# Copies of cache rows issued beside the weights' loads: in all four stages, or in the two feed-forward stages alone

## The chip, the cores and the metric

The kernel runs on one core of a Trainium2 chip. The metric is the device time of one execution in microseconds (us). The core's engines work side by side, each through its own list of instructions in order: TensorE (PE in the profile, its weight loads PEld), VectorE (DVE), ScalarE (ACT), GpSimd (POOL) and SyncE (SP), which here issues every DMA.

## What is computed

One inference step of a two-layer decoder, in float32: 512 new tokens of a prompt and one new token for each of 8 sample sequences, 520 columns in all, model width 1024.

```python
for i in range(DEPTH):                 # 2 layers
    x += mixer[i % 2](rmsnorm(x))      # 0: gated DeltaNet, 1: dilated window attention
    x += square(relu(rmsnorm(x) @ w_up)) @ w_down
# outputs: x, new states, and the key/value caches moved on by one row
bufs.append(jnp.concatenate([buf, new_rows], axis=1)[:, -keep:])
```

The last line is what the change is about. The sample sequences' caches (windows of 128, 512 and 1024 rows, 8 sequences, 8 KB a row) are outputs too: all old rows but the dropped one go unchanged from an input in DRAM to an output in DRAM, and one new row is added to each.

## The kernel before

The program has four stages in a row: `gdn` (the gated DeltaNet mixer), `mlp0` (feed-forward), `dsw` (dilated attention), `mlp1` (feed-forward). Activations stay on the chip with the model dimension on the partitions. Every projection takes a weight tile of 512 KB from DRAM (`raw`, L145, three buffers), which ScalarE rounds to `whi` (L130) and VectorE subtracts to `wlo` (L131), two buffers each; TensorE then runs three matmuls for each of the 8 blocks of the contraction (L164 to L166), in two halves of 260 columns, each in one of two PSUM buffers `mm`. A half is read out by an eviction (L762 and L896 are two of them) before its buffer is used again. A tile is thus 48 matmuls.

The copies of cache rows are a generator, `kept_rows` (L87): each is one DMA from DRAM to DRAM of up to 104 rows (832 KB; the rests are 704, 760 and 184 KB), 136 in all. After every weight load, `weights` draws from it:

```python
nc.sync.dma_start(raw, c[:, j : j + m].rearrange("(k p) n -> p k n", p=P))
self.owed += PACE[self.stage]
while self.owed >= 1:
    self.owed -= 1
    next(self.kept, None)
```

`owed` starts at -16, so the first 16 loads have no copy beside them, and every later one has one until the 136 are issued. After the last stage `for _ in K.kept: pass` (L1369) issues what is left, before the output is stored (`store_x`, L311).

In `gdn` the work goes by 8 pairs of heads, p = 0 to 7. For each pair a matrix has to be inverted. `decay` makes it on VectorE (E, L603). `invert` writes E's 32x32 blocks to DRAM (L629, four DMAs), loads them in another layout (Ft, L632), runs 31 steps of two small instructions on GpSimd (L638, L641), writes the result (L642) and loads it back (L646, four DMAs, into the tile `held`). `merge` joins the blocks, and begins on VectorE:

```python
nc.vector.transpose(T64[0:32, :, 0:32], Uf[0:32, :, 0:32])            # L653
nc.vector.transpose(T64[32:64, :, 32:64], Uf[32:64, :, 32:64])
nc.vector.transpose(T2[64:96], Uf[64:96, :, 64:96])
```

While that runs, the pair before is scanned (L713 to L743), its gates are projected (two tiles, evicted at L762), and its sample part (sks L820, sut L830, son L846) and its normalised output (osb L866, then otr L871) are made; `out_proj` (evicted at L896) adds earlier pairs to x. The order of instructions on each engine isn't the written one: a scheduler makes it, from a model of each instruction's and DMA's time; functions marked `urgent` and the DMAs in them come first where they can.

Of the kernel before, what the change touches and what calls it, by code (L numbers as in the profile page):

```python
# [43 lines left out]
MM = 2  # L44
OHB = 8
DOUT = {8: ((0,), (1, 2))}
PACE = dict(gdn=1, mlp0=1, dsw=1, mlp1=1)


class Common:  # L50


    def __init__(self, ctx, tc, I, O):
        self.tc, self.nc, self.I, self.O = tc, tc.nc, I, O
        nc = self.nc
        self.cst = ctx.enter_context(tc.tile_pool(name="cst", bufs=1))
        self.wp = ctx.enter_context(tc.tile_pool(name="wp", bufs=3))
        self.tp = ctx.enter_context(tc.tile_pool(name="tp", bufs=2))
        self.dp = ctx.enter_context(tc.tile_pool(name="dp", bufs=2, space=DRAM))
        self.pm = ctx.enter_context(tc.tile_pool(name="pm", bufs=2, space=PSUM))  # L60

        n = KT * T
        base = self.cst.tile([P, n + 2 * P + 4 * KT + SMALL], F32, name="base")
        split = self.cst.tile([P, 2 * n], F32R, name="split")
        self.x, self.xh, self.xl = (t.rearrange("p (k t) -> p k t", k=KT) for t in (base[:, :n], split[:, :n], split[:, n:]))
        self.ident, self.ones = base[:, n : n + P], base[:, n + P : n + 2 * P]
        self.gains = base[:, n + 2 * P : n + 2 * P + 4 * KT]
        self.small, self.places, self.used = base[:, n + 2 * P + 4 * KT :], {}, 0
        make_identity(nc, self.ident)
        nc.vector.memset(self.ones, 1.0)  # L70
        self.kept, self.owed, self.stage = self.kept_rows(), -16, "gdn"
        self.gain = {}
        for i, n in enumerate(("norm_mix", "norm_mlp")):
            self.gain[n] = self.gains[:, i * 2 * KT : (i + 1) * 2 * KT].rearrange("p (l k) -> p l k", l=2)
# [58 lines left out]
    def weights(self, cols, nk=KT):  # L133
# [4 lines left out]
        for c in cols:  # L138
            for j in range(0, c.shape[1], step):
# [5 lines left out]
# [3 lines that stand above are left out]
# [1263 lines left out]
```

## Time and profile before

| | us |
|---|---|
| median of 3 runs | 2148.9 (2146.82 to 2150.51) |
| the profiled execution, its own time | 2152.49 |
| its span, from the first to the last instruction | 2150.7 |
| TensorE busy in the span | 1972.8 (92%) |
| VectorE busy | 1319.7 (61%) |
| ScalarE busy | 892.5 (41%) |
| GpSimd busy | 500.4 (23%) |

By its first and last DMAs, `gdn` ends at about 790 us, `mlp0` at about 1130, `dsw` at about 1765, and `mlp1` goes to the end. The copies are issued from 153.9 to 1280.5 us: 49 in `gdn`, 64 in `mlp0`, 23 in `dsw`. To read the profile: a busy share is an average over stages with different limits, so the stretches are read one by one; an engine's idle time is put down to what ended it ("<-"); the granted clock of TensorE was 0.954 of full speed over the span.

### The profile page before, as it was taken

The page shows a single profiled execution, that of the slowest core. Times are in us where ns is not written, and L with a number is a line of the kernel's source. Part 1 is how long each engine was busy: PE and PEld are TensorE (multiplying, and loading weights), DVE is VectorE, ACT ScalarE, POOL GpSimd, SP SyncE. Part 2 cuts the span into 40 slices and gives each one's busy share as a digit, 9 for nine tenths or more (in the row PEclk, how much of TensorE's full clock was granted, in tenths as well). Part 3 has the DMA queues.
Part 4 walks back from the last instruction along what each step waited for, and adds up shares of the span by engine and source line. Part 5 has one row for each costly group of instructions (what it writes and reads, how often), then busy time and mean ns, then how long its engine had stood idle before and what let it go on. Part 6 is the DMA issues. An engine that isn't in the chain of part 4 may idle for free. (4 is left out here: it accounts for less than half of the span.)

```text
span 2150.7 us, 41729 instructions
## 1 busy us (share of the span) xinstructions
PE 1972.8 (92%) x16436; PEld 1937.4 (90%) x16436; DVE 1319.7 (61%) x3301; ACT 892.5 (41%) x2391; POOL 500.4 (23%) x749
## 2 busy tenths in 40 slices
PE   8959867977968789999999999999999989999998
PEld 7858867977968689999999999999999989999998
DVE  4746766956956575454454667666766784454444
ACT  4525433444434352323244545554555443233231
POOL 1162334444344230000001223322332340000000
PEclk8979988989989789999999999999999999999999
DMA  5534554746844538766765774453454333333332
GB/s 139 101 88 134 145 134 135 225 142 167 250 136 134 190 113 281 253 232 230 251 232 204 240 235 131 119 149 99 119 136 133 114 96 89 98 89 91 97 89 70
DMA packets 416277, 328.55 MB, mean 153 GB/s; under 512 B 48408, under 2 KB 404568, under 8 KB 413896
## 3 DMA queue, kind: packets, MB, share of 16 engines
q1 hardware_dynamic: 416080, 325.88, 50.4%
q8 instruction: 129, 2.11, 0.4%
q14 instruction: 68, 0.56, 0.1%
HBM read 302.19 MB, written 132.83 MB: 202 GB/s over the span
## 5 line engine op out<-in xcount | busy, mean ns | idle before, releaser
L164 PE MATMUL mm<-split,whi 128*128 128x260 f32 (+1 forms) x2960 | 861.7, 291 | 22.0 <-DVE base L848 17.4
L166 PE MATMUL mm<-split,wlo 128*128 128x260 f32 (+1 forms) x2960 | 849.1, 287 | 20.3 <-DVE wlo L131 20.3
L165 PE MATMUL mm<-split,whi 128*128 128x260 f32 (+1 forms) x2960 | 846.5, 286 | 1.1 <-DVE split L178 1.1
L164 PEld LDWEIGHTS mm<-split,whi 128*128 128x128 f32 (+1 forms) x2960 | 564.2, 191 | 24.5 <-DVE base L848 17.5
L166 PEld LDWEIGHTS mm<-split,wlo 128*128 128x128 f32 (+1 forms) x2960 | 563.1, 190 | 23.3 <-DVE wlo L131 22.5
L165 PEld LDWEIGHTS mm<-split,whi 128*128 128x128 f32 (+1 forms) x2960 | 564.3, 191 | 2.1 <-DVE split L178 1.5
L130 ACT CAST whi<-raw 128x1024 fp32r<-128x1024 f32 (+1 forms) x273 | 285.4, 1045 | 503.5 <-PE mm L165 484.2
L131 DVE TENSOR_TENSOR wlo<-raw,whi 128x1024 fp32r<-128x1024 f32 (+1 forms) x273 | 336.5, 1233 | 196.9 <-ACT whi L130 188.0
L166 PE MATMUL mm<-hh,wlo 128*128 128x260 f32 x1024 | 289.1, 283 | 0.0
L165 PE MATMUL mm<-hl,whi 128*128 128x260 f32 x1024 | 288.4, 282 | 0.0
L164 PE MATMUL mm<-hh,whi 128*128 128x260 f32 x1024 | 287.9, 282 | 0.0
L165 PEld LDWEIGHTS mm<-hl,whi 128*128 128x128 f32 x1024 | 192.7, 188 | 0.0
L166 PEld LDWEIGHTS mm<-hh,wlo 128*128 128x128 f32 x1024 | 192.6, 188 | 0.0
L164 PEld LDWEIGHTS mm<-hh,whi 128*128 128x128 f32 x1024 | 192.3, 188 | 0.0
L346 DVE TENSOR_TENSOR t<-mm,bc 128x260 f32<-128x260 f32 x128 | 54.8, 428 | 153.1 <-PE mm L166 153.1
L190 POOL TENSOR_TENSOR acc<-acc,sq 128x260 f32<-128x260 f32 x42 | 37.0, 889 | 380.3 <-ACT sq L189 379.9
L638 POOL TENSOR_TENSOR fs<-Ft,held 128x60 f32<-128x60 f32 (+24 forms) x248 | 90.3, 364 | 112.1 <-DMA Ft<-D 93.4
L130 ACT CAST hh<-q 128x260 fp32r<-128x260 f32 x128 | 52.5, 410 | 121.6 <-DVE q L333 121.6
L641 POOL TENSOR_TENSOR held<-held,fs 128x60 f32<-128x60 f32 (+24 forms) x248 | 90.4, 364 | 19.4
L131 DVE TENSOR_TENSOR hl<-q,hh 128x260 fp32r<-128x260 f32 x128 | 54.9, 429 | 57.1 <-ACT hh L130 57.1
L164 PE MATMUL mm<-onh,whi 128*128 128x260 f32 x256 | 85.2, 336 | 2.8 <-DVE ET L618 2.2
L839 POOL TENSOR_TENSOR ub<-ub,base 128x1024 f32<-128x1024 f32 x16 | 32.7, 2044 | 216.7 <-DMA ub<-Du 201.6
(378 smaller groups left out, 3273.9 us busy)
## 6 DMA issues: line engine op xcount, KB each, us to landing
out_dram<-in_cache_kv_w_dram SPq DMA_DIRECT2D x112, 832.0 KB
raw<-in_dsw_w_in_dram SPq DMA_DIRECT2D x72, 512.0 KB
raw<-in_mlp_w_up_dram SPq DMA_DIRECT2D x64, 512.0 KB
raw<-in_mlp_w_down_dram SPq DMA_DIRECT2D x64, 512.0 KB
raw<-in_gdn_w_in_dram SPq DMA_DIRECT2D x48, 512.0 KB
S<-in_state_gdn_dram SPq DMA_DIRECT2D x16, 512.0 KB
raw<-in_gdn_w_out_dram SPq DMA_DIRECT2D x16, 512.0 KB
ub<-Du SPq DMA_DIRECT2D x16, 512.0 KB
```

The costliest lines, as they stand in the source:

```text
L130: nc.scalar.copy(hi, src)
L131: nc.vector.tensor_tensor(lo, src, hi.bitcast(F32), ALU.subtract)
L164: nc.tensor.matmul(ps[:m], lhsT=w[0][:, k, :m], rhs=xh[:, s], start=k == 0, stop=False)
L165: nc.tensor.matmul(ps[:m], lhsT=w[0][:, k, :m], rhs=xl[:, s], start=False, stop=False)
L166: nc.tensor.matmul(ps[:m], lhsT=w[1][:, k, :m], rhs=xh[:, s], start=False, stop=k == nk - 1)
L190: nc.gpsimd.tensor_tensor(acc[:, s], acc[:, s], t, ALU.add)
L346: nc.vector.tensor_tensor(t, ps, r2[:, s], ALU.mult)
L638: nc.gpsimd.tensor_tensor(tmp[:, :m, :n], Ft[:, None, j + 1 :, j].to_broadcast([P, m, n]), Uo[:, :m, j : j + 1].to_broadcast([P, m, n]), A ...
L641: nc.gpsimd.tensor_tensor(Uo[:, :m, j + 1 :], Uo[:, :m, j + 1 :], tmp[:, :m, :n], ALU.add)
L839: nc.gpsimd.tensor_tensor(ub, ub, kqs[:, :, 0:1].to_broadcast([P, NS, P]), ALU.mult)
```

## The change

Two numbers change. `gdn` and `dsw` draw no copies, and `owed` starts at 0.

```diff
-PACE = dict(gdn=1, mlp0=1, dsw=1, mlp1=1)
+PACE = dict(gdn=0, mlp0=1, dsw=0, mlp1=1)
...
-        self.kept, self.owed, self.stage = self.kept_rows(), -16, "gdn"
+        self.kept, self.owed, self.stage = self.kept_rows(), 0, "gdn"
```

The two feed-forward stages have 64 loads each, so 128 copies are issued beside loads and 8 at the end. The scheduler makes another order from this, on all engines. Three places follow.

SP at the end of the program, before the change (`raw` is a weight tile, `yt` a block of the output):

```order
L145 DMA raw<-in_mlp_w_up_dram 128x8x128 x8
L145 DMA raw<-in_mlp_w_down_dram 128x8x128 x8
L311 DMA out_dram<-yt 128x1024 x4
L311 DMA out_dram<-yt 8x1024
L1407 UNCONDITIONAL_BRANCH
```

and now:

```order
L145 DMA raw<-in_mlp_w_down_dram 128x8x128
L97 DMA out_dram<-in_cache_kv_w_dram 16x13312 x7
L311 DMA out_dram<-yt 128x1024
L97 DMA out_dram<-in_cache_kv_w_dram 16x13312
L311 DMA out_dram<-yt 128x1024
L97 DMA out_dram<-in_cache_kv_w_dram 16x11264
L311 DMA out_dram<-yt 128x1024 x2
L311 DMA out_dram<-yt 8x1024
```

Seven copies now follow the last load, and two more stand between the stores of the output.

VectorE in `gdn`, at the merge of pair 7 (`sz<-zt,mm` is the eviction of a gate half, `wlo` a weight split), before:

```order
L844 TENSOR_TENSOR base<-base 128x16
L762 SCALAR_TENSOR_TENSOR sz<-zt,mm 128x260
L848 TENSOR_SCALAR base<-son 128x16
...
L131 TENSOR_TENSOR wlo<-raw,whi 128x1024
L219 TENSOR_TENSOR base<-base 128x24
L762 SCALAR_TENSOR_TENSOR sz<-zt,mm 128x260
L653 STREAM_TRANSPOSE held<-held 32x8x32
L654 STREAM_TRANSPOSE held<-held 32x8x32
```

and now:

```order
L823 TENSOR_TENSOR base<-base,held 128x8
L653 STREAM_TRANSPOSE held<-held 32x8x32
L826 TENSOR_TENSOR base<-base 128x16
L654 STREAM_TRANSPOSE held<-held 32x8x32
L827 TENSOR_TENSOR base<-base 128x16
L762 SCALAR_TENSOR_TENSOR sz<-zt,mm 128x260
L655 STREAM_TRANSPOSE T_7894<-held 32x256
L844 TENSOR_TENSOR base<-base 128x16
L131 TENSOR_TENSOR wlo<-raw,whi 128x1024
```

The transposes of the merge have moved ahead of the sample part's last steps, of a weight split and of both evictions.

VectorE at the merge of pair 5 (`base<-base,mm` is an eviction of the output projection), before:

```order
L896 TENSOR_TENSOR base<-base,mm 128x260
L827 TENSOR_TENSOR base<-base 128x16
L844 TENSOR_TENSOR base<-base 128x16
L896 TENSOR_TENSOR base<-base,mm 128x260 x2
L848 TENSOR_SCALAR base<-son 128x16
L653 STREAM_TRANSPOSE held<-held 32x8x32
```

and now:

```order
L896 TENSOR_TENSOR base<-base,mm 128x260
L653 STREAM_TRANSPOSE held<-held 32x8x32
L827 TENSOR_TENSOR base<-base 128x16
L654 STREAM_TRANSPOSE held<-held 32x8x32
L896 TENSOR_TENSOR base<-base,mm 128x260
L844 TENSOR_TENSOR base<-base 128x16
L655 STREAM_TRANSPOSE T_6151<-held 32x256
L896 TENSOR_TENSOR base<-base,mm 128x260
L131 TENSOR_TENSOR wlo<-raw,whi 128x1024
```

Here L653 has moved ahead of L844 and of two evictions. In pair 3 it moves ahead of one weight split and one eviction L762, in pair 6 ahead of L728, L596, L743, four small instructions and two evictions L896; in pair 4 it moves behind L844 and one weight split, and there E stands behind one weight split and three convolution steps (L525) that it stood ahead of. In pairs 0, 1 and 2 it keeps its place.

## Rows read from the trace of the kernel before

**Rows 1.** Busy time in four stretches: us, PE, PEld, DVE, ACT, POOL (instructions); PEclk, DMA share, GB/s

```profile
150.00:300.00 150.00, 119.92 (x1032) 115.77 (x1033) 94.56 (x282) 61.59 (x180) 57.19 (x129) 0.85 0.51 134
...
850.00:900.00 50.00, 50.00 (x420) 50.00 (x420) 24.57 (x43) 15.17 (x26) 0.00 (x0) 1.00 0.68 238
...
1200.00:1250.00 50.00, 49.96 (x416) 49.35 (x414) 30.89 (x98) 27.41 (x90) 18.31 (x11) 1.00 0.81 244
...
1850.00:1900.00 50.00, 50.00 (x420) 50.00 (x419) 23.50 (x42) 17.09 (x31) 0.00 (x0) 1.00 0.33 96
```

**Rows 2.** Who waited for whom: us in total, times, longest

```profile
DVE held L653 <- DMA held<-D: 91.0, 7, 19.6
```

**Rows 3.** VectorE in order of time, L653 of pairs 3, 5, 6, 7: start, us

```profile
371.92 0.43 DVE L653 STREAM_TRANSPOSE held<-held 32x256 f32<-32x256 f32 x1 [9.95 <-DMA held<-D]
...
535.81 0.43 DVE L653 STREAM_TRANSPOSE held<-held 32x256 f32<-32x256 f32 x1 [14.13 <-DMA held<-D]
...
617.54 0.43 DVE L653 STREAM_TRANSPOSE held<-held 32x256 f32<-32x256 f32 x1 [18.54 <-DMA held<-D]
...
702.30 0.43 DVE L653 STREAM_TRANSPOSE held<-held 32x256 f32<-32x256 f32 x1 [11.19 <-DMA held<-D]
```

**Rows 4.** TensorE in order of time, after its idle time in pairs 3 to 7

```profile
377.21 1.97 PE L871 MATMUL otr<-base,osb 128*128 128x128 f32 x8 [8.93 <-DVE osb L866]
...
452.15 0.58 PE L846 MATMUL son<-base 128*128 128x16 f32 x2 [11.57 <-DVE base L844]
...
538.93 0.58 PE L166 MATMUL mm<-split,wlo 128*128 128x260 f32 x1 [11.37 <-DVE wlo L131]
...
619.64 0.38 PE L830 MATMUL sut<-base 128*16 128x128 f32 x1 [18.04 <-DVE base L823]
...
706.28 1.97 PE L871 MATMUL otr<-base,osb 128*128 128x128 f32 x8 [12.44 <-DVE osb L866]
```

**Rows 5.** SP's DMA issues in order of time, pairs 1, 3 and 6

```profile
138.98 0.56 SPq L632 DMA_DIRECT2D Ft<-D  x1
...
325.70 1.82 SPq L629 DMA_DIRECT2D D<-E  x4
327.62 0.40 SPq L145 DMA_DIRECT2D raw<-in_gdn_w_in_dram  x1
328.06 0.59 SPq L97 DMA_DIRECT2D out_dram<-in_cache_kv_w_dram  x1
328.89 0.60 SPq L632 DMA_DIRECT2D Ft<-D  x1
...
558.20 2.37 SPq L796 DMA_DIRECT2D S<-in_state_gdn_dram  x2
562.35 2.69 SPq L629 DMA_DIRECT2D D<-E  x4
...
568.19 0.59 SPq L632 DMA_DIRECT2D Ft<-D  x1
```

**Rows 6.** GpSimd in order of time, the first step on Ft of pairs 1, 3, 6

```profile
148.79 0.25 POOL L638 TENSOR_TENSOR fs<-Ft,held 128x31 f32<-128x31 f32 x1 [9.53 <-DMA Ft<-D]
...
338.56 0.26 POOL L638 TENSOR_TENSOR fs<-Ft,held 128x31 f32<-128x31 f32 x1 [8.74 <-DMA Ft<-D]
...
580.55 0.25 POOL L638 TENSOR_TENSOR fs<-Ft,held 128x31 f32<-128x31 f32 x1 [12.99 <-DMA Ft<-D]
```

**Rows 7.** VectorE in order of time, weight splits ahead of L653, pairs 3 and 7

```profile
360.10 1.23 DVE L131 TENSOR_TENSOR wlo<-raw,whi 128x1024 fp32r<-128x1024 f32 x1 [2.38 <-ACT whi L130]
...
689.39 1.23 DVE L131 TENSOR_TENSOR wlo<-raw,whi 128x1024 fp32r<-128x1024 f32 x1 [0.16 <-ACT zt L761]
```

**Rows 8.** SP's DMA issues at the end

```profile
2091.09 17.73 SPq L145 DMA_DIRECT2D raw<-in_mlp_w_down_dram  x4
2142.35 4.08 SPq L311 DMA_DIRECT2D out_dram<-yt  x5
```

**Rows 9.** Busy time of one stretch at the end, columns as in rows 1

```profile
2144.00:2146.00 2.00, 1.00 (x10) 0.57 (x7) 1.37 (x2) 0.89 (x2) 0.00 (x0) 1.00 1.02 408
```

## The prediction

> **What bounds the kernel now.** I read the time by stage first, then who waits for whom, then single stretches in order of time.
>
> By stage: in the feed-forward stages TensorE never stops. A stretch of 50 us holds 420 matmuls, 0.119 us each, both in the first feed-forward stage, where a copy goes out beside each load, and in the second, where none does [rows 1]. The DMA engines are 0.68 busy there with copies and 0.33 without, and nobody waits. The first stage (gated DeltaNet, some 790 us) is different: TensorE is busy 119.92 of 150 us in the row shown [rows 1]. What is won or lost must be looked for there, and at the very end.
>
> Waits of the first stage: VectorE waits 91.0 us, seven times, for `held<-D` at L653 [rows 2]. L653 is the first instruction of a pair's merge. Before it lies a chain: E (VectorE), four writes to DRAM (L629), the load of Ft (L632), 62 small GpSimd steps, a write (L642), four loads (L646). VectorE takes its instructions in order, so whatever stands behind L653 waits too, and TensorE soon runs dry. At L653 of pairs 3, 5, 6 and 7 the waits are 9.95, 14.13, 18.54 and 11.19 us [rows 3]; TensorE's idle times in pairs 3 to 7 are 8.93, 11.57, 11.37, 18.04 and 12.44 us [rows 4]: 62 us. So a pair lasts as long as its chain, plus the work that the order puts between L653 and the next E. Two things change it: how long the chain takes, and what stands ahead of L653.
>
> **The change part by part.**
>
> *The chain without copies.* 49 copies leave the first stage. What they cost the chain is bounded by the chain's own transfers. From Ft's issue to the first GpSimd step it takes 9.67 us in pair 3 (328.89 to 338.56), with a weights' load and a copy issued just before it; 9.81 us in pair 1 (138.98 to 148.79), before the first copy of the kernel; and 12.36 us in pair 6 (568.19 to 580.55), the longest of pairs 1 to 7 [rows 5, 6]. From the first write of E to Ft's issue it is 3.19 us in pair 3 and 5.84 in pair 6 [rows 5]. Lower bound: pairs 1 and 3 say a copy costs nothing, 0. Upper bound: six pairs, all as bad as pair 6, and copies the only reason: 6 x (2.69 + 2.65) = 32 us. The mean between pair 3 and pair 6 over six pairs is 16; but in pair 6 two loads of state, 512 KB each, are issued 4 us ahead of E [rows 5], and they stay. I take half, **-8 us**. What follows, 33.4 us in pair 3 from the first GpSimd step to L653 (338.56 to 371.92) [rows 3, 6], is GpSimd's steps for the most part and stays.
>
> The Trainium skill (DMA: Bandwidth & Descriptors, "Queues, rings and completion order") has each DMA engine consume the descriptors of a queue in ring order, so a Ft issued behind a copy would start only after it. Pair 3 against pair 1 does not show that, pair 6 may. By the rule, with one copy of 2.1 us (priced below) ahead of Ft in each of pairs 3 to 7, this term would be -10.5, and the total 2.5 us lower.
>
> *The order of work.* Nothing in the diff says so, but the order on VectorE is made by a scheduler that reckons with the DMA queue, and without copies it puts L653 earlier in pairs 3, 5, 6 and 7 and later in pair 4. Where it is earlier, work that kept TensorE going during the chain now waits for it. `mm` has two PSUM banks, so TensorE gets two halves beyond the last eviction that stands ahead of L653. With t0 the start of L653:
> - Pair 7. Before, the weight split wlo (start 689.39) and two evictions L762 stand ahead of L653 [rows 7], TensorE finishes both gate tiles and waits only at `otr`, from 693.84 to t0 + 3.98 [rows 3, 4]. Now they stand behind: 48 matmuls (2 halves of 24, 5.7 us) cannot run. wlo is the eighth instruction from L653 on, ready at about t0 + 3.5 (eight durations of 0.2 to 1.2 us), and 5.7 us later `otr` comes: t0 + 9.2, so +5.2.
> - Pair 5. Before, TensorE waits from 527.56 to t0 + 3.12 for wlo. Now L844 and two evictions L896 stand behind L653. It stops after 12 matmuls of the output projection, at about 521.0, and 6.5 us of matmuls (55) follow after about t0 + 1.4: t0 + 7.9, so +4.8.
> - Pair 6. Eight instructions with 3.4 us in all (among them L596, 1.3 us) and two evictions come behind L653; TensorE stands 12 matmuls earlier and gets to `sut` at t0 + 5.5 in place of t0 + 2.10: +3.4.
> - Pair 3. wlo (360.10) and one L762 come behind L653 [rows 7]; 46 matmuls, 5.5 us, follow from t0 + 2.5: t0 + 8.0 in place of t0 + 5.29: +2.7.
> - Pair 4. L844 and wlo come ahead of L653, which frees some 12 matmuls (-1.3), but E itself moves behind one wlo and three convolution steps, up to 4 us of VectorE; between -1.3 and +2.7 I take +1.
>
> Sum **+17 us**. Bounds: 0, if what moved runs while VectorE would have kept TensorE waiting anyway; +19 with pair 4 at its worst. I take it nearly whole, as TensorE has no other long idle time after these waits to catch up in.
>
> *The dilated-attention stage* loses 23 copies. In a stretch of it in which they run, TensorE is busy 49.96 of 50 us [rows 1], so there is nothing to win: **0**; the order there changes by a few places, which I bound by 2 us either way, one gap of TensorE of the smallest kind in [rows 3, 4] (L653 to `sut`, 2.10).
>
> *The second feed-forward stage* gets 64 copies. The first one has the same load and copy pattern and the same 420 matmuls in 50 us [rows 1]: **0**. The cover is the DMA engines' free third; if it were gone, the loads would come late at wlo.
>
> *The end.* 136 copies, 128 loads: eight copies have no load. One copy goes beside the last load (the load ends at 2108.8 on SP) and six follow it, 33 us before the first store of the output [rows 8]: done by then, as 7 x 2.1 us is 15. Two stand between the stores of the output on SP. The price of a copy: (238 - 96) GB/s for (0.68 - 0.33) of the engines [rows 1], so 406 GB/s with all; 832 KB take 2.1 us, 704 KB 1.8. The stores are issued from 2142.35 on [rows 8], and in their last microseconds the engines are full, 1.02 at 408 GB/s [rows 9]. So the two copies delay the end by 3.9 us; not below 0, and with 2 us for their own landing at most 6. **+4 us**.
>
> Sum: -8 + 17 + 0 + 0 + 4 = +13. The profiled execution took 2152.49 us (its span 2150.7, and 1.8 around it), so 2165.5; the median shown is 3.6 lower, which gives **2162 us**.
>
> **Rivals.**
> - *The moved work costs nothing (faster).* What moves behind L653 runs beside VectorE's square roots up to L866, in which TensorE waits 2.1 to 5.3 us now. For: that wait is real [rows 3, 4]. Against: the moved work is 5.5 to 6.5 us in three pairs, more than that wait. The point from which it decides: a moved work of no more than these 2.1 to 5.3 us a pair, with a chain gain above 8 us. With a gain of 12, between my 8 and the mean of 16: -12 + 0 + 4 = -8, 2141 us.
> - *The chain gets as short as the scheduler reckons (no change).* If the copies were all of pair 6's excess, the waits shrink by 20 to 25 us in all, which pays for +17 and +4: 2145 to 2149 us. The skill's ring order, at full effect on L629 and Du as well, points this way. Against: pair 3.
> - *The copies hold up the second feed-forward stage (slower still).* A load behind a copy comes late at its split. It decides once the DMA engines have no free time left. Against: the equal 420 matmuls [rows 1]. Were each of the 64 splits that follow late by a tenth of a copy's 2.1 us, that is 13 us more: 2175.
>
> **How the numbers follow.** This kernel's runs can tell about 0.2%, 4.3 us, from no change. The forecast, slower by 13, has 0.6, and the third rival 0.05: slower 0.65. The second rival and the small sums around it: 0.18 same. The first: 0.17 faster. The range reaches down to 2144, where the chain gains most of its bound, and up to 2174, with the moved work at +19, the chain at 0 and the end at 6.
>
> **What would show it.** Right: VectorE's waits at L653 of pairs 3, 5, 6 and 7 longer than before, with TensorE idle about 14 us or more there; Ft still 9.5 to 11 us from issue to GpSimd; 420 matmuls per 50 us in both feed-forward stages; the end some 4 us later after the last eviction. Wrong: Ft and L629 faster by 3 us a pair; L653 waits under 8 us; or matmuls of the second feed-forward stage waiting for wlo.

## The result, and the profile after

| | us | against the kernel before, 95% interval |
|---|---|---|
| before, median | 2147.95 (2146.82 to 2150.51) | |
| the change, median | 2158.84 (2157.68 to 2160.51) | 1.0050 [1.0032, 1.0067] |
| the change, profiled execution | 2158.45, span 2156.7 | |

Slower by 0.5%, 10.9 us between the medians. The two profiled spans lie only 6.0 apart, because the profiled execution of before was itself 4.5 above its median; so single traces are used below for where time goes, and medians for how much.

**By stage.** The same instruction in both traces, first of before, then of the change: the first eviction of the first feed-forward stage (L333), and weight splits (L131) late in that stage, early in the second feed-forward stage and at its end (columns: start, duration, engine, line, operation, output and input, idle time ahead of it and what ended it):

```profile
785.60 0.42 DVE L333 SCALAR_TENSOR_TENSOR q<-mm,r 128x260 f32<-128x260 f32 x1
...
1163.16 1.23 DVE L131 TENSOR_TENSOR wlo<-raw,whi 128x1024 fp32r<-128x1024 f32 x1 [2.43 <-ACT whi L130]
...
1808.18 1.23 DVE L131 TENSOR_TENSOR wlo<-raw,whi 128x1024 fp32r<-128x1024 f32 x1 [2.04 <-ACT whi L130]
...
2130.22 1.23 DVE L131 TENSOR_TENSOR wlo<-raw,whi 128x1024 fp32r<-128x1024 f32 x1
```

```profile
792.98 0.42 DVE L333 SCALAR_TENSOR_TENSOR q<-mm,r 128x260 f32<-128x260 f32 x1
...
1170.79 1.23 DVE L131 TENSOR_TENSOR wlo<-raw,whi 128x1024 fp32r<-128x1024 f32 x1 [2.44 <-ACT whi L130]
...
1808.34 1.23 DVE L131 TENSOR_TENSOR wlo<-raw,whi 128x1024 fp32r<-128x1024 f32 x1 [1.11 <-PE mm L166]
...
2131.55 1.22 DVE L131 TENSOR_TENSOR wlo<-raw,whi 128x1024 fp32r<-128x1024 f32 x1
```

The change is 7.4 us behind when the first stage is over, 7.6 at the end of the first feed-forward stage, 0.2 after the attention stage, 1.3 at the last split. The first stage loses, the feed-forward stages keep their pace, the attention stage gives back (how much of that is the change is measured below), and the rest of the 6.0 comes behind the last split.

The feed-forward stages of the change, both with a copy beside each load now (window view; columns as in [rows 1]):

```profile
850.00:900.00 50.00, 50.00 (x420) 50.00 (x419) 24.20 (x42) 13.32 (x20) 0.00 (x0) 1.00 0.67 234
1850.00:1900.00 50.00, 50.00 (x420) 50.00 (x419) 24.32 (x43) 16.58 (x30) 0.00 (x0) 1.00 0.70 247
```

420 matmuls in 50 us in both, as in [rows 1]: 64 more copies hold nothing up there.

**The first stage.** VectorE's waits at L653 of pairs 3 to 7 in the change; [rows 3] has four of them before:

```profile
370.45 0.43 DVE L653 STREAM_TRANSPOSE held<-held 32x256 f32<-32x256 f32 x1 [13.18 <-DMA held<-D]
...
452.76 0.43 DVE L653 STREAM_TRANSPOSE held<-held 32x256 f32<-32x256 f32 x1 [16.00 <-DMA held<-D]
...
534.38 0.43 DVE L653 STREAM_TRANSPOSE held<-held 32x256 f32<-32x256 f32 x1 [15.57 <-DMA held<-D]
...
613.96 0.43 DVE L653 STREAM_TRANSPOSE held<-held 32x256 f32<-32x256 f32 x1 [16.55 <-DMA held<-D]
...
697.22 0.43 DVE L653 STREAM_TRANSPOSE held<-held 32x256 f32<-32x256 f32 x1 [14.30 <-DMA held<-D]
```

And TensorE's idle times there, which answer to [rows 4]:

```profile
373.22 0.58 PE L166 MATMUL mm<-split,wlo 128*128 128x260 f32 x1 [8.10 <-DVE wlo L131]
...
454.42 0.62 PE L786 MATMUL sst<-base 128*128 128x24 f32 x2 [14.23 <-DVE base L848]
...
536.04 0.61 PE L846 MATMUL son<-base 128*128 128x16 f32 x2 [13.99 <-DVE base L844]
...
619.10 0.38 PE L830 MATMUL sut<-base 128*16 128x128 f32 x1 [15.62 <-DVE base L823]
...
699.53 0.58 PE L846 MATMUL son<-base 128*128 128x16 f32 x2 [12.01 <-DVE base L844]
```

Pair 4's, which [rows 3] does not have, was 13.93 us before, and its L653 started at 450.84. So VectorE waits longer at L653 in four pairs of five (not in pair 6), although every L653 but pair 4's starts earlier than before. TensorE's idle time is 64.0 us against 62.4 [rows 4]: hardly more. So the lost 7 us are not in these waits alone.

**The end.** SyncE from the first store on (answering to [rows 8]):

```profile
2143.82 0.36 SPq L311 DMA_DIRECT2D out_dram<-yt  x1
2144.22 0.51 SPq L97 DMA_DIRECT2D out_dram<-in_cache_kv_w_dram  x1
2144.84 0.60 SPq L311 DMA_DIRECT2D out_dram<-yt  x1
2145.49 0.51 SPq L97 DMA_DIRECT2D out_dram<-in_cache_kv_w_dram  x1
2146.11 1.86 SPq L311 DMA_DIRECT2D out_dram<-yt  x3
```

From the first store to the end of the span it is 12.9 us (2143.82 to 2156.7), before 8.35 (2142.35 to 2150.7): +4.5.

### The profile page after: what moved, and what is told of

The parts are those of the page before. It is cut to its first block, busy times and chain, and to the rows that moved or that the text cites. A ratio compares the mean times of both kernels' runs of the same rounds, so it can differ in the third digit from the quotient of the medians.

```text
span 2156.7 us, 41701 instructions
## 1 busy us (share of the span) xinstructions
PE 1973.8 (92%) x16436; PEld 1941.1 (90%) x16436; DVE 1323.4 (61%) x3301; ACT 895.6 (42%) x2391; POOL 500.6 (23%) x749
## 3 DMA queue, kind: packets, MB, share of 16 engines
q1 hardware_dynamic: 416080, 325.88, 50.7%
## 5 line engine op out<-in xcount | busy, mean ns | idle before, releaser
L164 PEld LDWEIGHTS mm<-split,whi 128*128 128x128 f32 (+1 forms) x2960 | 564.6, 191 | 26.6 <-DVE base L848 20.2
L131 DVE TENSOR_TENSOR wlo<-raw,whi 128x1024 fp32r<-128x1024 f32 (+1 forms) x273 | 342.8, 1256 | 154.9 <-ACT whi L130 111.2
L131 DVE TENSOR_TENSOR hl<-q,hh 128x260 fp32r<-128x260 f32 x128 | 54.9, 429 | 57.0 <-ACT hh L130 57.0
L839 POOL TENSOR_TENSOR ub<-ub,base 128x1024 f32<-128x1024 f32 x16 | 34.2, 2138 | 204.1 <-DMA ub<-Du 160.4
```

Of the source, the lines that this page charges most:

```text
L131: nc.vector.tensor_tensor(lo, src, hi.bitcast(F32), ALU.subtract)
L164: nc.tensor.matmul(ps[:m], lhsT=w[0][:, k, :m], rhs=xh[:, s], start=k == 0, stop=False)
L839: nc.gpsimd.tensor_tensor(ub, ub, kqs[:, :, 0:1].to_broadcast([P, NS, P]), ALU.mult)
```

## The experiments

"The run without copies at the end" is e3, the base of several others.

**The parts alone: e1, e2, e3, e5.** The first stage alone (e1): copies by a count for each stage.

```diff
-PACE = dict(gdn=0, mlp0=1, dsw=0, mlp1=1)
+LEFT = dict(gdn=0, mlp0=64, dsw=23, mlp1=49)
...
-                self.owed += PACE[self.stage]
-                while self.owed >= 1:
-                    self.owed -= 1
-                    next(self.kept, None)
+                if self.left[self.stage] > 0:
+                    self.left[self.stage] -= 1
+                    next(self.kept, None)
```

> No copies in the first stage, but the 23 copies of the attention stage stay where they were (beside its first 23 loads), 64 beside the first feed-forward stage's loads, 49 beside those of the second, none after the last load. Forecast theory (the chain gains 8 us, the order of work costs 17): +9 us against the kernel before, and in the trace the weight splits of the first feed-forward stage 7 to 9 us later than before. Rival 'the chain pays for all': 0 or less, these splits at most 1 us later. Rival 'moved work costs nothing': -8 to -12 us.

The attention stage alone (e2), from the kernel before:

```diff
-PACE = dict(gdn=1, mlp0=1, dsw=1, mlp1=1)
+PACE = dict(gdn=1, mlp0=1, dsw=0, mlp1=1)
```

> The kernel before with only the attention stage's 23 copies taken away; they go beside the first 23 loads of the second feed-forward stage. The first stage and the end are those of before. Forecast theory: 0 (2 us either way). Rival from the two profiles: the weight splits were 7.5 us later than before at the first feed-forward stage's end and only 0.2 us later at the second's start, so the attention stage without copies is 6 to 7 us shorter: 2141 to 2143 us. Third possibility, the profiled execution of before was 4.5 us above its median for another reason: -2 to -3 us.

No copies after the last load (e3), from the change:

```diff
-PACE = dict(gdn=0, mlp0=1, dsw=0, mlp1=1)
+PACE = dict(gdn=0, mlp0=1.125, dsw=0, mlp1=1)
```

> The changed kernel, but eight loads of the first feed-forward stage take two copies, so none is left after the last load. Forecast theory: 3.9 us shorter than the change (two copies of 1.8 to 2.1 us stood between the stores), so 2155 us; the last matmul at the same time as in the change. Rival: the stores are slow at the end anyway, 0 to 1 us shorter.

The change once more (e5), no edit:

> The changed kernel once more, beside the others. Forecast theory: its own parts, first stage about +7 (measured alone), attention stage -2, end +4: +9 us against the kernel before, and 4 us more than the run without copies at the end; from the first store of the output to the end of the span 12 to 13 us in place of 8. Rival: the end is worth nothing and the change stands at +4 to +5.

| | median, us | before, measured beside it | ratio, 95% interval |
|---|---|---|---|
| e1, first stage alone | 2152.17 | 2145.68 | 1.0032 [1.0022, 1.0042] |
| e2, attention stage alone | 2143.34 | 2145.68 | 0.9991 [0.9982, 1.0000] |
| e3, both, without the end | 2150.24 | 2145.68 | 1.0020 [1.0011, 1.0029] |
| e5, all of the change | 2161.38 | 2149.99 | 1.0047 [1.0032, 1.0062] |

The parts add up: 0.32% - 0.09% = 0.23%, and e3, which has both, gives 0.20%. From there to the change (0.47 and 0.50%) is the end: 0.27 to 0.30%, 5.8 to 6.4 us by these ratios, 4.5 to 4.7 in the traces (from first store to end 13.06 us in e5, 8.35 before, 7.97 in e3). "The chain pays for all" and "moved work costs nothing" fall with e1; "the end is worth nothing" falls with e3 against e5. The attention stage is worth about 2 us, 4 at most, not the 7.4 by which the first two profiles drew level there (7.6 behind at its start, 0.2 after it).

**What e1, e2, e3, e5 and two more say of the chain and the order.** Each pair can be cut in two: from E's first write (L629) to L653, the chain; and from L653 to the next pair's first write (in pair 7 to the first L333 of the next stage), where the order of work tells. Means over executions that have the first stage of before (before, e2, e9) and that of the change (the change, e1, e3, e5, e12), in us:

| pair | chain, with copies | without | | after L653, with | without | |
|---|---|---|---|---|---|---|
| 3 | 45.7 | 44.6 | -1.1 | 29.2 | 34.4 | +5.2 |
| 4 | 48.7 | 48.4 | -0.3 | 36.6 | 33.0 | -3.6 |
| 5 | 48.1 | 48.2 | +0.1 | 26.6 | 28.8 | +2.1 |
| 6 | 55.2 | 50.7 | -4.5 | 33.8 | 36.0 | +2.2 |
| 7 | 50.8 | 47.3 | -3.5 | 84.4 | 92.5 | +8.1 |
| sum | | | **-9.3** | | | **+14.0** |

(e9 and e12 differ from these two first stages in one place of pair 7, below.) No part of the sums hangs on one run: the chain's sum lies between 247.9 and 249.1 with copies and between 236.4 and 240.6 without; what follows L653 between 209.2 and 212.1 with, and between 223.1 and 227.3 without. Over pairs 3 to 6 the two nearly cancel (-5.8 and +5.9); what is left is pair 7. A part of what e1 lost lies ahead of this table: the first write of pair 3's E comes at 324.8 to 325.7 us with copies and at 325.7 to 330.5 without.

Half of what the copies cost the chain is to be seen on SyncE. Before, pairs 6 and 7, just ahead of the loads of `held`:

```profile
611.70 0.68 SPq L97 DMA_DIRECT2D out_dram<-in_cache_kv_w_dram  x1
613.59 1.32 SPq L646 DMA_DIRECT2D held<-D  x3
...
696.23 0.54 SPq L97 DMA_DIRECT2D out_dram<-in_cache_kv_w_dram  x1
698.07 1.82 SPq L646 DMA_DIRECT2D held<-D  x4
```

and the same in the change:

```profile
612.14 1.81 SPq L646 DMA_DIRECT2D held<-D  x4
...
695.39 1.81 SPq L646 DMA_DIRECT2D held<-D  x4
```

A copy stands there in pairs 6 and 7 alone. From the first load's issue to L653 it is 3.95 and 4.23 us in them before ([rows 3]), 1.82 and 1.83 in the change, and 1.6 to 1.9 in pairs 3 to 5 of either. In e2 and e9, which have these copies too, it is 3.73 to 4.28 us. So a copy issued 1.8 to 1.9 us ahead of a small load cost it 2.1 to 2.4 us here, about the 2.1 that the prediction worked out for the copy's own transfer.

**Order put back by hand: e4, e7, e6.** In pair 7 the gates ahead of the merge (e4; in e7 the same for pairs 3, 5, 6 and 7), from e3:

```diff
-                        nc.vector.scalar_tensor_tensor(szs[:, v, s], t, 1.0, ps, ALU.add, ALU.mult)
+                        self.sz.append(nc.vector.scalar_tensor_tensor(szs[:, v, s], t, 1.0, ps, ALU.add, ALU.mult).ins)
...
+            early = p == last
+            if early:
+                A.gates()
...
-                with tc.issue_after(A.conv0), tc.issue_after(A.flip0):
+                with tc.issue_after(A.conv0), tc.issue_after(A.flip0), tc.issue_after(A.sz[1] if early else A.flip0):
...
-            if p:
+            if p and not early:
                 A.gates()
```

> As the run without copies at the end, but in pair 7 the two gate projections (weight split, matmuls, evictions L762) stand ahead of the merge's transposes on VectorE, where two of the four evictions and one split stood before. Forecast theory: pair 7's term of the order of work was +5.2 us, so about 5 us shorter than the run without copies at the end: 2150 us. Reading of the two profiles: TensorE also runs on a granted clock of 0.5 to 0.6 after the long idle of pair 7 (0.79, 0.53 and then 1.00 before), so up to 9 us shorter: 2146 us. Rival: pair 7's order costs nothing, the lower clock comes anyway: 0 to 1 us.

> As the run without copies at the end, but in pairs 3, 5, 6 and 7 all four evictions of the gates and their splits stand ahead of the merge's first transpose. Forecast theory: 8 us or more shorter than the run without copies at the end. Reading of the run with pair 7 alone (2 us longer, not shorter): TensorE's work is only exchanged, evictions of the output projection fall behind the merge in turn, so 0 to +6 us.

The merge without its raised priority (e6), from e3:

```diff
-"merge": 2000
+"merge": 0
```

> As the run without copies at the end, but the merge is recorded without its raised priority; the scheduler then puts its first transpose on VectorE behind two more weight splits in pair 3 and one more in pairs 4, 5 and 7, about the places of the kernel before or later. Forecast theory (what stands behind that transpose costs, the chain without copies is some 10 us shorter over pairs 3 to 7): the first stage gets most of the 15 to 17 us of order back, 8 us or more shorter than the run without copies at the end: 2142 us or less. Rival 'the order is not what costs': within 3 us of that run. Rival 'later merges only move the wait to the next pair': the same or a few us longer.

e4: 2152.63 us against 2145.68, 1.0041 [1.0028, 1.0054]. e7: 2164.54 against 2149.99, 1.0052 [1.0032, 1.0071]; its six executions spread from 2155.37, the profiled one, to 2167.01. e6: 2181.77 against 2149.99, 1.0141 [1.0126, 1.0157]. All above e3's 1.0020. None gives the forecast's gain: what is put ahead of L653 pushes other work behind it (in e4 eight evictions of the output projection, and TensorE waits 12.1 us at pair 7's merge as in the change). In e7's profile pair 7 itself did get its time back, and pairs 5 and 6 lost it; this is taken up below. In e6 the price is elsewhere. VectorE's row of E in pair 3, before and in e6:

```profile
323.52 0.60 DVE L603 SCALAR_TENSOR_TENSOR E<-kk,base,ET 128x128 f32<-128x128 f32 x2
```

```profile
346.56 0.61 DVE L603 SCALAR_TENSOR_TENSOR E<-kk,base,ET 128x128 f32<-128x128 f32 x2
```

L653 of pair 2 comes 5 us later than before (293.34 and 288.24), E of pair 3 23 us later, and the later pairs don't win it back. The third rival had the sign, none the size; what holds E up was not followed further.

**Copies only up to pair 5: e8**, from e2 (the count of loads begins at 0):

```diff
-                self.owed += PACE[self.stage]
+                self.loads += 1
+                self.owed += 0 if self.stage == "gdn" and self.loads > 46 else PACE[self.stage]
```

> The run without copies in the attention stage alone, but in the first stage the copies stop after 46 loads: pairs 3 to 5 keep copies and order of the kernel before, pairs 6 and 7 have neither. From the pairs' times with and without copies: chain -4.3 in pair 6 and -3.6 in pair 7, what follows the merge +2.0 and +8.5: first stage +2 to +3 us, 2146 us. If the order's cost in pair 7 is only its granted clock, and that is chance: -4 to -6 us, 2139 us.

2153.79 against 2149.99, 1.0018 [1.0007, 1.0029]: 3.8 us with the attention stage's -1.9 in it, so 5.7 for what follows the last copy against the 2 to 3 worked out, and far from -4 to -6. That is nearly all of what e1 lost, though the chain of pairs 6 and 7 is 8.4 us shorter here as well (97.6 us of two pairs, 106.0 before). It isn't only these two pairs: in the trace one copy stands in pair 5's chain in place of four, and pair 5's stretch after L653 is already 30.6 us long (26.5 before).

**Order alone in pair 7: e9**, the kernel before with its copies:

```diff
-                nc.vector.transpose(T64[0:32, :, 0:32], Uf[0:32, :, 0:32])
+                self.first = nc.vector.transpose(T64[0:32, :, 0:32], Uf[0:32, :, 0:32]).ins
...
-                        nc.vector.scalar_tensor_tensor(szs[:, v, s], t, 1.0, ps, ALU.add, ALU.mult)
+                        with tc.issue_after(self.first) if p == last else nullcontext():
+                            nc.vector.scalar_tensor_tensor(szs[:, v, s], t, 1.0, ps, ALU.add, ALU.mult)
```

> The kernel before with all its copies; only the four evictions of pair 7's gates are held behind the first transpose of that pair's merge (two of the four stood ahead of it), as the change has them. So order alone, no copy moved. Forecast theory: pair 7's term, +5.2 us against the kernel before; from that transpose to the fifth split of the first feed-forward stage 98.5 to 102 us in place of 93.5 (102 in the runs without copies), TensorE on half its clock for longer between 700 and 745. Rival 'the work is only exchanged': 0 to 2 us.

2151.38 against 2149.28, 1.0003 [0.9991, 1.0015]: the gates' evictions behind L653 cost nothing by themselves. But the scheduler did not make the change's order of it. VectorE in e9:

```profile
699.21 0.43 DVE L653 STREAM_TRANSPOSE held<-held 32x256 f32<-32x256 f32 x1 [11.51 <-DMA held<-D]
...
702.34 1.22 DVE L867 TENSOR_TENSOR osb<-osb,base 128x1024 f32<-128x1024 f32 x1
```

The scaling of the output (L867 here, L866 in the kernel before) still follows L653 by 3.1 us, as before (2.7), since the sample part's steps up to L848 kept their place ahead of L653; in the change it is 10.6. e9 excludes the evictions alone as the cause, not the order.

**The scaling brought forward: e12**, from e3:

```diff
-                        nc.vector.scalar_tensor_tensor(szs[:, v, s], t, 1.0, ps, ALU.add, ALU.mult)
+                        with tc.issue_after(pairs[p - 1].scaled) if p == QK_HEADS - 1 else nullcontext():
+                            nc.vector.scalar_tensor_tensor(szs[:, v, s], t, 1.0, ps, ALU.add, ALU.mult)
```

(`scaled` is the pair's L866.)

> As the run without copies at the end, but in pair 7 the four evictions of the gates stand on VectorE behind the scaling of pair 6's output (the instruction that ended TensorE's wait at its transposes before), so that scaling comes soon after the merge's first transpose: 2.7 us in the runs with copies in the first stage, 8.9 to 10.6 without. Everything up to the merge of pair 7 is as in that run. Forecast theory (what the order puts between the merge's first transpose and the next work of TensorE is lost): the scaling comes 3 to 4.5 us after the first transpose, 5 to 6 us shorter than the run without copies at the end, so level with the kernel before or up to 3 us shorter than it. Rival 'the gates are due anyway': the same as that run, +4 us against the kernel before. Rival 'the clock after the long wait decides': 2 us shorter at most, with matmuls 0.22 us apart from 710 to 740 all the same.

2153.32 against 2148.28, 1.0028 [1.0014, 1.0043]: no better than e3. The scaling came 6.2 us after L653 (703.78 and 697.55), not 3 to 4.5: the sample part's sum (L846) and the twelve steps of a square root stand between. But also with it earlier, pair 7 took 92.8 us from L653 to the next stage, as without. So it isn't that one instruction that decides. Nor was the clock what the third rival said: granted was 0.94 from 710 to 720 and 0.74 from 720 to 730, near e9's, and the time was lost all the same.

**TensorE's wait filled: e10 (from e3) and e11 (from e2).**

```diff
                 ps = K.bank("son")
+                for _ in range(64 if p == 6 else 0):
+                    nc.tensor.matmul(ps[:, :P], lhsT=ident, rhs=ident, start=True, stop=True)
```

> As the run without copies at the end, but 64 matmuls of 128x128 whose result nobody reads stand on TensorE in its wait at pair 7's merge, ahead of the sample part's matmul (L846 in the change) that ended that wait. The 24 like them at the kernel's start took 6.96 us, so 64 take 9.3 us at twice that rate; TensorE waits 10.6 to 12.0 us there without them. Theory that pair 7 loses its time to the granted clock after the wait (matmuls 0.22 us apart in place of 0.12 from 712 to 742): the clock stays up, 4 to 8 us shorter than the run without copies at the end. Rival 'the clock falls whatever TensorE does in that wait': the same within 2 us. Rival 'they come in the way of the twelve projection matmuls behind them': 1 to 3 us longer.

> The run without copies in the attention stage alone (copies in the first stage as before), with the same 64 matmuls in pair 7's wait. Clock theory: up to 5 us shorter than that run, 3 to 7 us under the kernel before. Rival: as that run, -2 us against the kernel before, or longer if the matmuls come in the way.

e10: 2167.32 against 2149.28, 1.0088 [1.0075, 1.0101]; e11: 2149.99, 1.0003 [0.9991, 1.0014]. TensorE in e10:

```profile
689.49 14.46 PE L847 MATMUL son<-base 128*128 128x128 f32 x128
...
727.90 1.12 PE L696 MATMUL vtr<-base,conv 128*128 128x128 f32 x4 [16.23 <-DVE ot L875]
```

The 64 matmuls took 14.5 us, not 9.3, at full clock (1.00 from 690 to 710), so they came in the way; and a new wait of 16.2 us followed, in which TensorE waited for VectorE, VectorE for ScalarE (12.6 us) and ScalarE for a store of the state (18.3 us). e10 therefore says little on the clock. e11 says more: its clock stayed up through the wait and fell to 0.59 and 0.50 in the two stretches of 10 us from 710 on, and the kernel won nothing. But in e11 the scheduler also put a third eviction and a weight split behind L653, so it is not e2 with the wait filled and nothing else.

## Why the prediction was right, and where it was not

**The sum and its signs held.** Forecast +13 (2162 by the median), measured +10.9. First stage +9 by -8 + 17; measured +6.5 between medians alone (e1, 0.22 to 0.42%), and by the table -9.3 + 14.0 over pairs 3 to 7. Attention stage 0 within 2; measured -2.3 (0.00 to -0.18%). Second feed-forward stage 0; +1.2 from its first split shown to its last (322.0 us before, 323.2 now). End +4 (bounds 0 to 6); 4.5 to 4.7 in the traces, 5.8 to 6.4 by the ratios; why these two differ was not followed.

**The chain: right in size, wrong in place.** The forecast had the copies cost at Ft and at L629, and let the stretch from GpSimd's first step to L653 "stay". Ft is as slow as ever: 8.9 us in pair 3, 11.1 to 11.8 in pairs 4 to 7 of the change (9.67 in [rows 5, 6], 11.0 to 12.4). The largest piece of the gain is in the stretch that should have stayed: two loads of `held` that stood behind a copy, 2.1 and 2.4 us, 4.5 of the 9.3. Only in pair 6 did something lie where the forecast had it: L629 to Ft took 4.02 us in the change (5.84 in [rows 5]), Ft to the first step 11.57 (12.36). By the means over the same executions these two pieces gave 3.5 us of the 9.3 in all pairs together, 2.7 of them in pair 6. So that -8 came out near the measured sum is in good part luck. The Trainium skill (DMA: Bandwidth & Descriptors, "Queues, rings and completion order") says that each DMA engine consumes descriptors in ring order. The trace agrees at L646, 2.1 and 2.4 us for a copy priced at 2.1; at Ft it does not show it (pair 3 took 9.67 us 0.8 us behind a copy, and 8.90 to 10.14 without one). The rule's -10.5 came nearer to the measured -9.3 than the forecast's -8, though it, too, was applied to Ft.

**The order: right in sum, not by pairs.** +5.2, -3.6, +2.1, +2.2, +8.1 against forecasts of 2.7, +1 (-1.3, and 2.3 for pair 4's late E, which in the table falls to pair 3: 5.0 and -1.3), 4.8, 3.4, 5.2. Pair 4 gave back more than reckoned, pairs 5 and 6 lost less and pair 7 lost more, so that the sum fits owes something to errors that cancel. For pairs 5 and 6, that a part of what moved runs while VectorE works down what stands behind L653, as the first rival had it, would explain it and was not tested. "TensorE idle about 14 us or more in pairs 3, 5, 6 and 7" came true in two of the four, and in pair 6, one of them, it was less than before. Pair 7 is the step that was mis-sized: +5.2 forecast, +8.1 measured. "48 matmuls, 5.7 us" took TensorE at full clock, and the account ended at `otr`. `otr` came 13.9 us after L653 in the change (711.10 and 697.22) and 10.2 to 11.9 in e1, e3 and e5, where the forecast had 9.2; and the pair is not over there. The scan of pair 7 begins later still. Its first step on TensorE after the merge, before and in the change:

```profile
723.03 0.59 PE L713 MATMUL pk<-S,kq 128*128 128x256 f32 x2
```

```profile
742.11 0.76 PE L713 MATMUL pk<-S,kq 128*128 128x256 f32 x2
```

20.7 us after L653 before, 44.9 in the change. In between lie the gates that came behind L653, the sample part's `sks` that the scheduler put ahead of the scan, and a TensorE at half its clock. The granted clock, before and in the change (last three columns: PEclk, DMA share, GB/s):

```profile
710.00:720.00 10.00, 9.95 (x131) 8.95 (x128) 5.22 (x10) 3.62 (x9) 4.45 (x2) 1.00 0.77 246
720.00:730.00 10.00, 6.98 (x56) 6.55 (x54) 4.45 (x10) 2.40 (x6) 2.55 (x2) 1.00 0.66 173
730.00:740.00 10.00, 10.00 (x47) 9.91 (x48) 2.72 (x13) 5.04 (x14) 0.00 (x0) 0.50 0.34 115
```

```profile
710.00:720.00 10.00, 8.90 (x87) 7.82 (x88) 8.43 (x14) 2.78 (x8) 4.70 (x2) 0.58 0.79 244
720.00:730.00 10.00, 10.00 (x71) 9.24 (x71) 1.70 (x4) 2.03 (x5) 0.00 (x0) 0.50 0.59 159
730.00:740.00 10.00, 10.00 (x49) 10.00 (x48) 2.02 (x12) 6.24 (x17) 0.00 (x0) 0.50 0.00 0
```

At 1.2 GHz (0.50) the projection's matmuls stand 0.22 us apart (720.33 and 720.55, say), at 2.4 GHz (1.00) 0.12. In the first two of these stretches e1, e3 and e5 show 0.64 to 0.93 and then 0.50 to 0.67; e2 and e9, with copies, 1.00 and then 0.79 to 0.80.

**Pair 7 counted out.** The whole stretch from L653 of pair 7 to the first L333, before, in the change and in e7 (window view, columns as in [rows 1]):

```profile
702.30:785.60 83.30, 66.69 (x478) 61.19 (x478) 60.76 (x163) 36.03 (x103) 29.57 (x22) 0.77 0.43 133
```

```profile
697.22:792.98 95.76, 78.57 (x520) 73.32 (x520) 69.77 (x177) 38.42 (x106) 30.66 (x22) 0.73 0.36 107
```

```profile
704.69:789.28 84.59, 68.51 (x462) 63.92 (x463) 57.69 (x151) 35.96 (x101) 29.48 (x22) 0.73 0.34 98
```

TensorE's idle time in this stretch hardly differs: 16.6 to 19.0 us in the three executions with copies (before, e2, e9), 17.2 to 19.9 in the five without (the change, e1, e3, e5, e12). What grew is its busy time, from 64.9 to 67.0 us with copies to 72.0 to 78.6 without. There is more work in the stretch (478 to 493 matmuls with copies, 515 to 528 without), and by the clock's records more of it ran at 0.50 (25.9 to 29.7 us with, 32.6 to 46.3 without). An estimate from these records, with a busy us at 0.50 counted as half a us of work, splits the +8.1 into about 3.5 us of work that came behind L653, about 4.8 us of lower clock and nothing of idle time. So of the forecast's +5.2, work that runs behind L653, some 3.5 is found; the larger part of the +8.1 is the lower clock, which the forecast put at nothing without a reason.

e7 and e12 tell the two parts apart a little. In e7's profile the gates, the scaling and `otr` of pair 7 stand ahead of its L653 (`otr` by 13.1 us), and 84.6 us follow, as with copies, although the mean clock is the change's; but pair 5, behind whose L653 ten evictions of the output projection stand in place of e3's two, takes 42.3 us after it in place of 28.8, and pair 6 takes 40.1 in place of 36.0. In e12 the clock was near e9's in the first 20 us from 710 on, and pair 7 lost its 8 us all the same. So work that was put ahead of one merge was paid for at another, and the clock right after the wait did not decide alone.

**What stays open.** That pair 7 loses some 8 us after its L653 without copies is shown in five executions, and the split of them above is an account of where the time lies, not a test. What lowers the clock there is not shown: e4 and e12 changed one piece of the order each and won nothing, e7 moved the loss to other pairs, e10 and e11 kept the clock up in the wait only. No kernel here has the order of before without the copies, so that the order causes the whole loss is argued, not shown.

## What to carry over

Moving DMAs that nobody waits for is not free when a scheduler reckons with them: compare the order of the compute engines first, and price what changes place there. A chain that got shorter by 9.3 us gave nothing here, as what followed it got longer by 14.0; so take each pair or tile to its last instruction, not to the end of the first wait, and count idle time, work and clock apart. And keep leftovers out of the tail: two copies between the output's stores cost about as much here as the whole first stage lost.

No kernel tried beats both by more than the measurement can tell; the nearest is e2, with the copies taken from the attention stage alone (0.9991 [0.9982, 1.0000]).

## What was not expected of the hardware

GpSimd's two long instructions of the sample part stop VectorE. In the change, VectorE at the scaling in pair 7, then GpSimd:

```profile
705.65 1.90 DVE L220 TENSOR_TENSOR base<-base 128x24 f32<-128x24 f32 x1
...
707.80 3.25 DVE L866 TENSOR_TENSOR osb<-osb,base 128x1024 f32<-128x1024 f32 x1
```

```profile
705.60 1.90 POOL L839 TENSOR_TENSOR ub<-ub,base 128x1024 f32<-128x1024 f32 x1 [14.94 <-DMA ub<-Du]
707.58 2.38 POOL L842 TENSOR_TENSOR S<-S,ub 128x1024 f32<-128x1024 f32 x1
```

L220 takes 0.18 us elsewhere and L866 1.23 (705.00 in the kernel before), so 1.7 and 2.0 us were spent standing behind L839 and L842. The Trainium skill (SBUF — State Buffer, "SBUF: two separate sides") has the two engines share a pair of ports under an exclusive lock: of a GpSimd instruction that reads the on-chip buffer and a VectorE one with two inputs there, the one that starts first blocks the other for its whole length. The trace agrees: L220 started 0.05 us after L839 and L866 0.22 us after L842. What is hit depends on half a us: L839 starts 8.4 us after L653 in the change and 8.9 in e3, where, with the same order, L866 started 0.03 us ahead of it and took 1.22; there L839 took 2.96 in place of 1.90, and L877, behind L866, 1.87 in place of 0.17. The two blocks are 3.7 us of the 13.9 between L653 and `otr` in the change's profiled execution, which is the difference from e3's 10.2.

Executions of nearly one order also differ in the first stage by as much as the change is worth there: from the first write of pair 3's E to the first L333 the change, e1, e3, e5 and e12 took 466.8, 462.7, 459.8, 465.7 and 464.5 us, those with copies 457.6 to 460.0. One profile of each would have shown anything from 0 to 9 us.
